# Gate and up products of a SwiGLU layer as seven block products instead of eight

## The chip, the cores and the metric

The kernel runs on one core of a Trainium2 chip. A core has a matrix engine (TensorE, in the profile PE, its weight loads PEld), three engines for element-wise work (VectorE or DVE, ScalarE or ACT, GpSimd or POOL), and queues that issue transfers (SP, and queues of ACT and POOL). Data lies in HBM, in the on-chip memory SBUF, and in PSUM, eight banks of 128 x 512 floats into which TensorE writes. The metric is the time of one execution on the device in microseconds (us).

## The reference

One decoder layer over 512 tokens of width 2048 in float32, then a norm:

```
h = rmsnorm(x, ln_mix);  proj = h @ w_in
mixed = [rmsnorm(stick_breaking(q, k, v)), rmsnorm(sliding_window(q, k, v, sinks))]
x = x + mixed @ w_out
h = rmsnorm(x, ln_ffn)
gate, up = split(h @ w_gate_up, 2)          # 2048 x 5632 each
x = x + (silu(gate) * up) @ w_down          # 5632 x 2048
out = rmsnorm(x, ln_final)
```

The change concerns the gate and up products and what lies around them; the attention groups are as they were.

## The kernel before

Every large product runs in three matmuls: both factors are split into a rounded part (hi) and the rest (lo), and hi x hi, hi x lo and lo x hi are added in PSUM. ScalarE writes hi (a copy, line 172 for weights), VectorE writes lo (a subtraction of hi from the raw value, line 173).

Weights come in slabs of 128 x 1024 from a queue. `step()` runs one group of three matmuls of the slab at its head; in the course of a slab it also loads the next two and splits the next one, so that transfers and splits lie under matmuls. `drain()` runs the queue to a mark, and `pull()` lets other work be woven in. `defer(n, fn)` runs a piece of work after n further groups. Loads go out through SP, pinned to written order; the order of the other engines' instructions is set by a scheduler that takes what is ready, with written order as priority. Each engine then takes its own instructions in that fixed order.

The stages: attention with its projections; the output projection in two halves (`add_outA`, `add_outB`), which leaves x2, the residual, in four column quarters in SBUF; then the feed-forward part. `h2_split(c)` transposes a quarter of x2 and splits it into hi and lo of the transposed tokens (lines 226 and 227). `add_up(n)` queues the gate and the up product of a group of 512 features (`add_wide`, lines 364 to 366: weight slab stationary, 512 tokens moving, 16 steps of contraction), reads the banks, applies the norm's factor per token and Silu, and splits the result (lines 896 to 906). `add_down(n)` multiplies the group before it with its down weights, and adds to x2 (line 916). The eleven groups alternate: up of group n, down of group n - 1. The last group's down product goes token tile by token tile, with the final norm behind it.

Of the kernel before, what the change touches and what calls it, by code (L numbers as in the profile page):

```python
# [8 lines left out]
F32 = mybir.dt.float32  # L9
# [28 lines left out]
def tile_hymba(ctx: ExitStack, tc: tile.TileContext, x, ln_mix, w_in, sb_norm, swa_norm,  # L38
# [7 lines left out]
    act = ctx.enter_context(tc.tile_pool(name="act", bufs=32))  # L46
    o8 = ctx.enter_context(tc.tile_pool(name="o8", bufs=2))
    v8 = ctx.enter_context(tc.tile_pool(name="v8", bufs=4))
    wp = ctx.enter_context(tc.tile_pool(name="wp", bufs=2))
    sm = ctx.enter_context(tc.tile_pool(name="sm", bufs=4))  # L50
    ps = ctx.enter_context(tc.tile_pool(name="ps", bufs=2, space=bass.MemoryType.PSUM))

# [83 lines left out]
    # Products with weights run from one queue of slabs [128, a, b] of a weight  # L136
    # (a*b = 1024), each split exactly in hi + lo ahead of its matmuls.
# [4 lines left out]
    def load(i):  # L142
# [4 lines left out]
        if sl["big"] is not None:  # L147
            # two slabs of one load
            if not sl["big"]:
                sl["big"].append(phase[1].tile([P, 2 * a, b], F32, tag="raw8", name="raw8", bufs=2))  # L150
# [31 lines left out]
    def step():  # L182
        """One group of matmuls of the queue; returns its time on the tensor engine."""
# [33 lines left out]
    carry = [0.0]  # L217

    def drain(mark=None):
        """To the end of slab number mark, or of the queue."""  # L220
# [23 lines left out]
    def row_bc(col, name):  # L244
# [6 lines left out]
        res = const.tile([P, S], F32, tag="rbc", name=name)  # L251
# [3 lines left out]
    # h^T = (x * g)^T, split  # L255
    h_hi = [None] * KT
    h_lo = [None] * KT
    XC = [(0, 256), (256, 256), (512, 512), (1024, 512), (1536, 512)]
# [13 lines left out]
    def h_make(kt):  # L272
# [4 lines left out]
        h_hi[kt] = act.tile([P, 512], F32R, tag="a", name="hhi")  # L277
        h_lo[kt] = act.tile([P, 512], F32R, tag="a", name="hlo")
# [48 lines left out]
    # queued products with features on the output partitions, 256 at a time  # L327
# [26 lines left out]
    # the same, 512 features at a time, in pairs of slabs of one load  # L354
# [30 lines left out]
    # V of the first head group, per key block [128 keys, head, hi | lo]  # L385
# [53 lines left out]
    def stack_two(src, r0, hi, lo):  # L439
        """[hi;hi] and [lo;lo] of the 64 rows of src from r0."""  # L440
# [581 lines left out]
```

## Time and profile before

| | |
|---|---|
| time, median of 3 runs | 2176.59 us (2175.39 to 2176.8) |
| profiled execution, first to last instruction | 2174.1 us; the page gives no other time of it |
| PE busy | 2156.3 us, 99% |
| DVE busy | 1040.6 us, 48% |
| ACT busy | 772.3 us, 36% |
| POOL busy | 131.1 us, 6% |
| moved by DMA | 208.18 MB, mean 96 GB/s |
| attention with its projections | about 0 to 590 us |
| end of output projection | about 725 us |
| gate, up and down products | about 725 to 2165 us |

Busy time is the union of an engine's instructions; matmuls overlap, so the pace of TensorE is read from the distance of their starts. A row of a group gives line, engine, operation, the output and inputs by the program's names, shapes and count, then the busy time in us with the mean of one in ns, and the time that the engine stood idle before them with what ended it. A row of a timeline gives start and duration in us.

### The profile page before, as it was taken

To read this page: it belongs to the slowest core of one execution; us is meant where nothing else is said; L and a number is where in the kernel's file an instruction comes from. 1 tells how busy PE (TensorE), PEld (TensorE's weight loads), DVE (VectorE), ACT (ScalarE), POOL (GpSimd) and SP (SyncE) were. 2 spreads that over 40 slices of the span, in tenths; PEclk is the share of its full clock that TensorE was granted. 3 is DMA by queue.
4 is the path that set the end of the run, shared out by engine and by line. 5 is a ranking of instruction groups with operands and counts; after the bars stand their busy time and mean duration, and the time that the engine had idled before them with its cause. 6 is when DMAs were issued, how large, how long until landed. Compare 5 with 4: busy or idle time off the path is not lost.

```text
span 2174.1 us, 24468 instructions
## 1 busy us (share of the span) xinstructions
PE 2156.3 (99%) x9930; PEld 1790.5 (82%) x9930; DVE 1040.6 (48%) x1521; ACT 772.3 (36%) x1277; POOL 131.1 (6%) x193
## 2 busy tenths in 40 slices
PE   8999999999999999999999999999999999999998
PEld 7888888988888888888888888888888888888886
DVE  4368888679834333433424334252333424334265
ACT  5347777468624322212222221222212222221232
POOL 0024444100100000000000000000000000000000
PEclk9999999999999999999999999999999999999999
DMA  5232221222333222222222222222222222222332
GB/s 182 90 88 59 68 68 59 78 77 79 136 116 115 69 97 97 97 97 97 97 97 97 97 97 97 97 97 97 97 97 97 97 97 97 97 97 97 107 126 78
DMA packets 136960, 208.18 MB, mean 96 GB/s; under 512 B 5072, under 2 KB 51216, under 8 KB 136720
## 3 DMA queue, kind: packets, MB, share of 16 engines
q1 hardware_dynamic: 136576, 205.54, 28.1%
q8 instruction: 78, 1.28, 0.2%
q0 software_dynamic: 176, 1.06, 0.1%
q14 instruction: 34, 0.28, 0.0%
q10 hardware_dynamic: 96, 0.02, 0.0%
HBM read 202.41 MB, written 4.19 MB: 95 GB/s over the span
## 4 chain that ended last, share of the span: by engine, by line
PE 98%; DVE 1%; ACT 0%; DMA 0%; issue 0%; SPq 0%; DVEq 0%
PE z L366 7%; PE z L364 7%; PE z L365 7%; PE m L337 4%; PE m L339 4%; PE m L338 4%; PE z L306 4%; PE z L305 4%; PE z L307 4%; PE m L305 4%; PE m L307 4%; PE o L366 4%; PE m L365 4%; PE m L366 4%; PE o L365 4%; PE o L364 4%
## 5 line engine op out<-in xcount | busy, mean ns | idle before, releaser
L173 DVE TENSOR_TENSOR wlo<-raw,whi 128x1024 fp32r<-128x1024 f32 x360 | 441.6, 1227 | 962.0 <-ACT whi L172 959.6
L172 ACT ACTIVATE whi<-raw 128x1024 fp32r<-128x1024 f32 x360 | 381.2, 1059 | 1152.6 <-PE o L365 325.9
L364 PE MATMUL z<-h2hi,whi 128*128 128x512 f32 x704 | 273.9, 389 | 0.0
L365 PE MATMUL z<-h2lo,whi 128*128 128x512 f32 x704 | 273.9, 389 | 0.0
L366 PE MATMUL z<-h2hi,wlo 128*128 128x512 f32 x704 | 273.9, 389 | 0.0
L337 PE MATMUL m<-hhi,whi 128*128 128x512 f32 x416 | 169.5, 407 | 0.9 <-DVE swv L227 0.9
L339 PE MATMUL m<-hhi,wlo 128*128 128x512 f32 x416 | 163.2, 392 | 0.0
L338 PE MATMUL m<-hlo,whi 128*128 128x512 f32 x416 | 163.2, 392 | 0.0
L365 PEld LDWEIGHTS z<-h2lo,whi 128*128 128x128 f32 x704 | 132.2, 188 | 27.5
L366 PEld LDWEIGHTS z<-h2hi,wlo 128*128 128x128 f32 x704 | 132.2, 188 | 27.4
L364 PEld LDWEIGHTS z<-h2hi,whi 128*128 128x128 f32 x704 | 132.2, 188 | 27.3
L364 PE MATMUL o<-h2hi,whi 128*128 128x512 f32 x352 | 137.1, 390 | 0.0
L364 PE MATMUL m<-h2hi,whi 128*128 128x512 f32 x352 | 137.1, 390 | 0.0
L366 PE MATMUL o<-h2hi,wlo 128*128 128x512 f32 x352 | 137.0, 389 | 0.0
L366 PE MATMUL m<-h2hi,wlo 128*128 128x512 f32 x352 | 136.9, 389 | 0.0
L365 PE MATMUL m<-h2lo,whi 128*128 128x512 f32 x352 | 136.9, 389 | 0.0
L365 PE MATMUL o<-h2lo,whi 128*128 128x512 f32 x352 | 136.9, 389 | 0.0
L305 PE MATMUL z<-whi,ah 128*128 128x512 f32 x320 | 124.5, 389 | 0.0
L306 PE MATMUL z<-wlo,ah 128*128 128x512 f32 x320 | 124.5, 389 | 0.0
L307 PE MATMUL z<-whi,al 128*128 128x512 f32 x320 | 124.5, 389 | 0.0
L339 PEld LDWEIGHTS m<-hhi,wlo 128*128 128x128 f32 x416 | 78.1, 188 | 17.7
L337 PEld LDWEIGHTS m<-hhi,whi 128*128 128x128 f32 x416 | 78.9, 190 | 11.0 <-PE z L745 1.1
(261 smaller groups left out, 3721.9 us busy)
## 6 DMA issues: line engine op xcount, KB each, us to landing
raw<-in_w_gate_up_dram SPq DMA_DIRECT2D x88, 1024.0 KB, 4.9
raw<-in_w_down_dram SPq DMA_DIRECT2D x40, 1024.0 KB, 5.1
raw<-in_w_in_dram SPq DMA_DIRECT2D x40, 512.0 KB, 3.5
raw<-in_w_in_dram SPq DMA_DIRECT2D x64, 256.0 KB, 3.2
raw<-in_w_out_dram SPq DMA_DIRECT2D x32, 512.0 KB, 3.6
x<-in_x_dram SPq DMA_DIRECT2D x4, 1024.0 KB, 6.8
raw<-in_w_down_dram SPq DMA_DIRECT2D x8, 512.0 KB, 6.1
out_dram<-x SPq DMA_DIRECT2D x16, 256.0 KB, 2.6
```

The source lines that it names most:

```text
L172: ih = A.activation(out=hi, in_=raw, func=AF.Copy)
L173: il = V.tensor_tensor(out=lo, in0=raw, in1=f(hi), op=ALU.subtract)
L305: mm(o, lhsT=lh[:, sl], rhs=hi[:, j, :], start=first, stop=False, skip_group_check=halves)
L306: mm(o, lhsT=lh[:, sl], rhs=lo[:, j, :], start=False, stop=False, skip_group_check=halves)
L307: mm(o, lhsT=ll[:, sl], rhs=hi[:, j, :], start=False, stop=(k == nslab * a - 1), skip_group_check=halves)
L337: mm(o, lhsT=wh, rhs=xh, start=(k == 0), stop=False)
L338: mm(o, lhsT=wh, rhs=xl, start=False, stop=False)
L339: mm(o, lhsT=wl, rhs=xh, start=False, stop=(k == KT - 1))
L364: mm(o, lhsT=wh, rhs=xh, start=(k == 0), stop=False)
L365: mm(o, lhsT=wh, rhs=xl, start=False, stop=False)
L366: mm(o, lhsT=wl, rhs=xh, start=False, stop=(k == KT - 1))
```

## The change

The matrix of tokens (512 x 2048) is cut into token halves and feature halves, the pair gate and up (2048 x 2 x 128 per unit of 128 features) into row halves and into gate and up. The 2 x 2 block product is formed from seven products of sums of blocks (the form of Winograd), named "1" to "7" and run in the order 1, 2, 5, 6, 3, 7, 4.

- Token side: `h2_split` now writes the transposed, scaled quarter unsplit (`xh`). `h_slab` forms the seven sums of token blocks for each of two slabs of 1024 features, some on VectorE and two on GpSimd, and `halves_of` splits each: hi of 256 tokens in columns 0 to 255, lo in 256 to 511 (`hc`). Slab 0 is made during the output projection, slab 1 during the first products.
- Weight side: a `Part` loads four blocks per unit (128 columns, 512 rows for each of two slabs), forms four sums of them on GpSimd (`sum`, two products ahead), splits each of the seven on ScalarE and VectorE (`split`, one ahead) and multiplies (`product`: 8 matmuls of 512 columns with hi, 8 of 256 columns with lo, into one bank). Unit 0 comes in two parts, one for each slab.
- `take` combines the seven banks in SBUF as they come, one product late; `finish` adds the halves (hi and lo columns) on GpSimd, applies factor and Silu, and stores 128 x 512 activations to HBM (`aT`).
- x2 goes to HBM (`x2s`) at the end of each quarter of the output projection, and comes back ahead of the down products, which now all follow the last unit. Activations are loaded by group and split again (`load_act`, `split_act`). The factor of the second norm is now in the activations.
- Tiles of 128 x 512 that were single are now held by fours (`act8`); pools of SBUF are closed and opened at the two borders of the stage.

The diff, cut to its core:

```diff
-    o8 = ctx.enter_context(tc.tile_pool(name="o8", bufs=2))
...
+    def act8(name, dt=F32R):
+        return act.tile([P, 4, 512], dt, tag="a8", name=name, bufs=8)
...
+    x2s = [dram.tile([P, NT, 512], F32, name=f"x2s{c}") for c in range(4)]
+    aT = [dram.tile([P, 4, 512], F32, name=f"aT{n}") for n in range(NFF // 4)]
+    xh = [None] * 4
+    hc = {}
...
     def h2_split(c):
+        xh[c] = (o8.tile([P, 4, 512], F32, tag="o8", name="xh") if c < 2 else e8("xh"))
         for k4 in range(4):
             kt = c * 4 + k4
             pb = pz()
             for t in range(NT):
                 nc.tensor.transpose(out=pb[:, t * P:(t + 1) * P], in_=x2[c][:, t, k4 * P:(k4 + 1) * P], identity=ident)
-            h2_hi[kt] = act.tile([P, 512], F32R, tag="a", name="h2hi")
-            h2_lo[kt] = act.tile([P, 512], F32R, tag="a", name="h2lo")
-            split_scaled(pb, gcol[:, 16 + kt:17 + kt], h2_hi[kt], h2_lo[kt])
+            V.scalar_tensor_tensor(out=xh[c][:, k4, :], in0=pb, scalar=gcol[:, 16 + kt:17 + kt], in1=rs1["b"],
+                                   op0=ALU.mult, op1=ALU.mult)
+    def halves_of(src, hl):
+        A.activation(out=hl[:, :, 0:256], in_=src, func=AF.Copy)
+        V.tensor_tensor(out=hl[:, :, 256:512], in0=src, in1=f(hl)[:, :, 0:256], op=ALU.subtract)
+    def h_blocks(s, a11, a21, a12, a22, stmp, new):
+        s1, s2 = stmp[:, 0], stmp[:, 1]
+        s4, s3 = s1, s2
+        def put(p, src):
+            hc[p, s] = new(p)
+            halves_of(src, hc[p, s])
+        put("1", a11)
+        yield
+        put("2", a12)
+        yield
+        V.tensor_tensor(out=s1, in0=a21, in1=a22, op=ALU.add)
+        put("5", s1)
+        yield
+        V.tensor_tensor(out=s2, in0=s1, in1=a11, op=ALU.subtract)
+        put("6", s2)
+        yield
+        G.tensor_tensor(out=s4, in0=a12, in1=s2, op=ALU.subtract)
+        put("3", s4)
+        yield
+        G.tensor_tensor(out=s3, in0=a11, in1=a21, op=ALU.subtract)
+        put("7", s3)
+        yield
+        put("4", a22)
+    def h_slab(s):
+        xa, xb = xh[2 * s], xh[2 * s + 1]
+        return h_blocks(s, xa[:, :, 0:256], xa[:, :, 256:512], xb[:, :, 0:256], xb[:, :, 256:512],
+                        e8("ssum").rearrange("p (u a) (h b) -> p u (a h) b", u=2, h=2),
+                        lambda p: act8("hca") if p not in "125" else
+                        side.tile([P, 4, 512], F32R, tag="s8", name="hcs", bufs=3) if s == 0 else
+                        ft("hct", [P, 4, 512], F32R, 3))
     def add_outB(c):
         def done(t, pb):
             xc = x2[c][:, t, :]
             V.scalar_tensor_tensor(out=xc, in0=pb, scalar=rstdB[:, t:t + 1], in1=xc, op0=ALU.mult, op1=ALU.add)
-            A.activation(out=tmp(name="junk"), in_=xc, func=AF.Square, accum_out=ss2[:, t, c:c + 1])
+            A.activation(out=junk, in_=xc, func=AF.Square, accum_out=ss2[:, t, c:c + 1])
             if t == NT - 1:
-                defer([6, 6, 38, 8][c], lambda: h2_split(c))
-                if c == 3:
-                    defer(9, rstd2_make)
+                dma(out=x2s[c], in_=x2[c])
+                if c < 3:
+                    defer(6, lambda: h2_split(c))
+                if c == 1:
+                    defer(12, lambda: list(h_slab(0)))
...
+    drain(outB0)
+    phase[0].close()
+    right = ExitStack()
+    side = right.enter_context(tc.tile_pool(name="side", bufs=1, side="right", reuse_waits="tile"))
+    drain()
...
+    class Part:
+        def __init__(self, unit, s0, s1):
+            self.u, self.s0, self.s1 = unit, s0, s1
...
+        def load(self, q):
+            r, c = int(q[0]) - 1, int(q[1]) - 1
+            raw = (wp.tile([P, 8, P], F32, tag="raw", name="raw", bufs=RAWB) if c == 0 else
+                   ft("raw2", [P, 8, P], F32, 3))
+            c0 = c * DFF + self.u.j * P
+            for s in range(self.s0, self.s1):
+                r0, k = s * 1024 + r * 512, 4 * (s - self.s0)
+                dma(out=raw[:, k:k + 4, :], in_=wgu[r0:r0 + 512, c0:c0 + P].rearrange("(a p) c -> p a c", p=P))
+            self.raw[q] = raw[:, 0:self.n, :]
+        def sum(self, p):
+            if p not in "5674":
+                return
+            t = ft("t", [P, 8, P], F32, 3)[:, 0:self.n, :]
+            a, b = {"5": ("12", "11"), "6": ("22", "T5"), "7": ("22", "12"), "4": ("21", "T6")}[p]
+            G.tensor_tensor(out=t, in0=self.raw[a], in1=self.t[b[1]] if b[0] == "T" else self.raw[b],
+                            op=ALU.subtract)
+            self.t[p] = t
+        def split(self, p):
+            src = self.t[p] if p in self.t else self.raw[{"1": "11", "2": "21", "3": "22"}[p]]
+            hi = wp.tile([P, 8, P], F32R, tag="whi", name="whi", bufs=2)[:, 0:self.n, :]
+            lo = wp.tile([P, 8, P], F32R, tag="wlo", name="wlo", bufs=2)[:, 0:self.n, :]
+            A.activation(out=hi, in_=src, func=AF.Copy)
+            V.tensor_tensor(out=lo, in0=src, in1=f(hi), op=ALU.subtract)
+            self.w[p] = hi, lo
+        def product(self, p):
+            if self.s0 == 0:
+                self.u.bank[p] = bank8()
+            b = self.u.bank[p]
+            hi, lo = self.w.pop(p)
+            for i in range(self.n):
+                x = hc[p, self.s0 + i // 4][:, i % 4, :]
+                mm(b, lhsT=hi[:, i, :], rhs=x, start=(self.s0 == 0 and i == 0), stop=False, skip_group_check=True)
+            for i in range(self.n):
+                x = hc[p, self.s0 + i // 4][:, i % 4, 0:256]
+                mm(b[:, 0:256], lhsT=lo[:, i, :], rhs=x, start=False,
+                   stop=(self.s1 == 2 and i == self.n - 1), skip_group_check=True)
+    class Unit:
+        def __init__(self, j):
...
+        def take(self, p):
+            b = self.bank
+            def plus(tile, bank, other):
+                V.tensor_tensor(out=tile, in0=bank, in1=other, op=ALU.add)
+                return tile
+            if p == "1":
+                self.w4 = e8("w4")
+                self.s1 = self.w4[:, 0, :]
+                A.activation(out=self.s1, in_=b["1"], func=AF.Copy)
+                self.c = e8("c4")
+            elif p == "2":
+                plus(self.c[:, 0, :], b["2"], self.s1)
+            elif p == "6":
+                self.u2 = plus(self.w4[:, 1, :], b["6"], self.s1)
+                self.u4 = plus(self.w4[:, 2, :], b["5"], self.u2)
+            elif p == "3":
+                plus(self.c[:, 2, :], b["3"], self.u4)
+            elif p == "7":
+                self.u3 = plus(self.w4[:, 3, :], b["7"], self.u2)
+                plus(self.c[:, 3, :], b["5"], self.u3)
+            elif p == "4":
+                plus(self.c[:, 1, :], b["4"], self.u3)
+                self.finish()
+        def finish(self):
+            g4 = e8("g4")
+            g, u, a = g4[:, 0, :], g4[:, 1, :], g4[:, 2, :]
+            G.tensor_tensor(out=g4[:, 0:2, :].rearrange("p a (h b) -> p (a h) b", h=2), in0=self.c[:, :, 0:256], in1=self.c[:, :, 256:512], op=ALU.add)
+            V.tensor_tensor(out=g, in0=g, in1=r2["b"], op=ALU.mult)
+            A.activation(out=g, in_=g, func=AF.Silu)
+            V.tensor_tensor(out=u, in0=u, in1=r2["b"], op=ALU.mult)
+            V.tensor_tensor(out=a, in0=g, in1=u, op=ALU.mult)
+            dma(out=aT[self.j // 4][:, self.j % 4, :], in_=a)
+    h2_split(3)
+    upper.close()
+    upper = ExitStack()
+    ff = upper.enter_context(tc.tile_pool(name="ff", bufs=1, reuse_waits="tile"))
...
...
+    first = {"1": ("11",), "2": ("21",), "5": ("12",), "6": ("22",)}
...
...
+    LD, SU = 7, 2
+    for n in range(LD):
+        ahead(n, "load")
+    for n in range(SU):
+        ahead(n, "sum")
+    ahead(0, "split")
...
+    for n, (pt, p) in enumerate(steps):
+        ahead(n + LD, "load")
+        ahead(n + SU, "sum")
+        ahead(n + 1, "split")
+        pt.product(p)
+        if n == 1:
+            late = h_slab(1)
+        if 2 <= n < 7:
+            next(late, None)
+            next(late, None)
+        if n == 7:
+            rstd2_make()
+        if taken:
+            u, q = taken.pop()
+            u.take(q)
+        if pt.s1 == 2:
+            taken.append((pt.u, p))
+    u, q = taken.pop()
+    u.take(q)
+    tc.keep_in_program_order(A.preload_act_table_set("natural_log_exp_and_others"))
+    upper.close()
+    right.close()
+    upper = ExitStack()
+    xp = upper.enter_context(tc.tile_pool(name="xp", bufs=1, reuse_waits="tile"))
+    side = upper.enter_context(tc.tile_pool(name="side2", bufs=1, side="right", reuse_waits="tile"))
...
+    def load_act(n):
+        raw = side.tile([P, GF, 512], F32, tag="ar", name="araw", bufs=2)
+        dma(out=raw, in_=aT[n])
+        acts[n] = raw
+    def split_act(n):
+        raw = acts[n]
+        ah = side.tile([P, GF, 512], F32R, tag="ah", name="ah", bufs=2)
+        al = side.tile([P, GF, 512], F32R, tag="al", name="al", bufs=2)
+        for h in range(2):
...
+            A.activation(out=ah[:, sl, :], in_=raw[:, sl, :], func=AF.Copy)
+            V.tensor_tensor(out=al[:, sl, :], in0=raw[:, sl, :], in1=f(ah)[:, sl, :], op=ALU.subtract)
+        acts[n] = ah, al
...
+    load_act(0)
+    split_act(0)
+    load_act(1)
+    for c in range(4):
+        x2[c] = xp.tile([P, NT, 512], F32, tag="x2", name="x2r", bufs=4)
+        nc.scalar.dma_start(out=x2[c], in_=x2s[c])
...
...
-    def add_up(n):
-        sg = [None] * GF
-        c0 = n * GF * P
-        def g_done(c, pb):
-            g = sg[c] = tmp(name="g")
-            V.tensor_tensor(out=g, in0=pb, in1=r2["b"], op=ALU.mult)
-            A.activation(out=g, in_=g, func=AF.Silu)
-        def u_done(c, pb):
-            if c == 0:
-                acts[n] = (o8.tile([P, GF, 512], F32R, tag="o8", name="ah"),
-                           phase[1].tile([P, GF, 512], F32R, tag="al", name="al", bufs=2))
-            ah, al = acts[n]
-            V.tensor_tensor(out=sg[c], in0=pb, in1=sg[c], op=ALU.mult)
-            A.activation(out=ah[:, c, :], in_=sg[c], func=AF.Copy)
-            V.tensor_tensor(out=al[:, c, :], in0=sg[c], in1=f(ah)[:, c, :], op=ALU.subtract)
-        add_wide(wgu, c0, next_four, g_done, h2T)
-        add_wide(wgu, DFF + c0, next_four, u_done, h2T)
     def add_down(n):
         for c in range(4):
             r0 = n * GF * P
             def done(t, pb, c=c):
                 xc = x2[c][:, t, :]
-                V.scalar_tensor_tensor(out=xc, in0=pb, scalar=r2["c"][:, t:t + 1], in1=xc,
-                                       op0=ALU.mult, op1=ALU.add)
+                V.tensor_tensor(out=xc, in0=pb, in1=xc, op=ALU.add)
             add_tok(lambda s, c=c: wdn[r0:r0 + GF * P, c * 512:(c + 1) * 512], GF // 2, 2, 512,
...
     def last_w(k2, c):
         raw = wp.tile([P, 2, 512], F32, tag="raw", name="raw", bufs=RAWB)
...
-        for e in range(2):
-            hi = act.tile([P, 512], F32R, tag="a", name="lhi")
-            lo = act.tile([P, 512], F32R, tag="a", name="llo")
-            A.activation(out=hi, in_=raw[:, e, :], func=AF.Copy)
-            V.tensor_tensor(out=lo, in0=raw[:, e, :], in1=f(hi), op=ALU.subtract)
-            lastw[2 * k2 + e, c] = (hi, lo)
-    # last norm: out = (x * g) * rstd
+        if k2 == 0:
+            lastw[c] = act8("lhi"), act8("llo")
+        hi, lo = (x[:, 2 * k2:2 * k2 + 2, :] for x in lastw[c])
+        A.activation(out=hi, in_=raw, func=AF.Copy)
```

More of the change, by code (lines that the diff above doesn't have):

```diff
@@ L250, in row_bc @@
                skip_group_check=True)
[L251 removed]
+        res = const.tile([P, S], F32, name=name)
         A.activation(out=res, in_=pb, func=AF.Copy)
@@ L965, in last_col @@
                 dma(out=o2d[t * P:(t + 1) * P, k * 512:(k + 1) * 512], in_=xc)
-    for n in range(1, NG):
-        add_up(n)
-        if n == NG - 1:
-            queue[-1]["post"] = last_up
+    for n in range(NG - 1):
+        if n == NG - 2:
             last_from = len(queue)
-        add_down(n - 1)
+        add_down(n)
     drain(last_from)
```

99 lines of the change are left out of this document (69 added, 30 removed).

## The prediction

> **What bounds the kernel now.** I read the page first, then the windows, the timelines of single engines, and the groups.
>
> ```profile
> span 2174.1 us, 24468 instructions
> PE 2156.3 (99%) x9930; PEld 1790.5 (82%) x9930; DVE 1040.6 (48%) x1521; ACT 772.3 (36%) x1277; POOL 131.1 (6%) x193
> PE 98%; DVE 1%; ACT 0%; DMA 0%; issue 0%; SPq 0%; DVEq 0%
> L173 DVE TENSOR_TENSOR wlo<-raw,whi 128x1024 fp32r<-128x1024 f32 x360 | 441.6, 1227 | 962.0 <-ACT whi L172 959.6
> L172 ACT ACTIVATE whi<-raw 128x1024 fp32r<-128x1024 f32 x360 | 381.2, 1059 | 1152.6 <-PE o L365 325.9
> L364 PE MATMUL z<-h2hi,whi 128*128 128x512 f32 x704 | 273.9, 389 | 0.0
> L364 PE MATMUL o<-h2hi,whi 128*128 128x512 f32 x352 | 137.1, 390 | 0.0
> L364 PE MATMUL m<-h2hi,whi 128*128 128x512 f32 x352 | 137.1, 390 | 0.0
> ```
>
> TensorE is the bound: 98% of the chain that ended last is its own. Lines 364 to 366 are the gate and up products, three matmuls of each kind, 3 x (704 + 352 + 352) = 4224. Their 389 ns overlap, so the pace must come from a stretch in which nothing else runs. The windows give it (columns: stretch, length, then busy time and count of PE, PEld, DVE, ACT, POOL, clock, DMA share, GB/s).
>
> ```profile
> 217.00:271.00 54.00, 54.00 (x272) 44.76 (x271) 47.42 (x83) 41.42 (x86) 22.31 (x33) 1.00 0.23 69
> 1000.00:1200.00 200.00, 200.00 (x884) 165.66 (x883) 77.89 (x85) 46.18 (x49) 0.00 (x0) 1.00 0.28 95
> 2170.00:2174.00 4.00, 0.00 (x0) 0.00 (x0) 0.00 (x0) 0.00 (x0) 0.00 (x0) 0.50 0.57 207
> ```
>
> 884 matmuls in 200 us are 226.2 ns each, at full clock. Gate and up therefore hold TensorE for 4224 x 0.2262 = 955.6 us. VectorE (DVE) is busy for 39% of that stretch and GpSimd (POOL) not at all.
>
> **TensorE's part of the change.** For each of the 44 units (128 gate and 128 up features) there are now seven products with 1024 of contraction. Each product is 8 matmuls of 512 columns (weight hi by token hi and lo) and 8 of 256 columns (weight lo by token hi). The narrow ones run in the shared projection of the sliding window's values.
>
> ```profile
> 411.00 0.28 PE L305 MATMUL m<-whi,hhi 128*128 128x256 f32 x1
> 411.12 0.28 PE L306 MATMUL m<-wlo,hhi 128*128 128x256 f32 x1
> ...
> 420.00 0.28 PE L305 MATMUL m<-whi,hhi 128*128 128x256 f32 x1
> 437.09 0.40 PE L338 MATMUL m<-hlo,whi 128*128 128x512 f32 x1
> 437.32 0.39 PE L339 MATMUL m<-hhi,wlo 128*128 128x512 f32 x1
> 437.55 0.28 PE L305 MATMUL m<-whi,hhi 128*128 128x256 f32 x1
> 437.67 0.28 PE L306 MATMUL m<-wlo,hhi 128*128 128x256 f32 x1
> ```
>
> From 411.00 to 420.00 lie 75 steps, 120 ns each, every one with its own weight load, and a change of width in between costs nothing. A product is 8 x 0.2262 + 8 x 0.120 = 2.77 us, a unit 19.39 us, all units 853.1 us. TensorE's term is 853.1 - 955.6 = -102.5 us. The down products (2112 matmuls) keep their number and shape.
>
> The Trainium skill, "TensorE: Matmul & The Clock Gate", section "Back-to-back issue gap", has N/2.4 + 2.5 ns for one matmul; that estimate is 215.8 and 109.2 ns here and would make this term -110.8 us. The rows are 10 ns slower each, and they decide.
>
> **What VectorE and GpSimd get.** Per unit VectorE subtracts seven weight slabs (L173's shape, 1.227 us), reads PSUM seven times (one bank, one tile of SBUF) and multiplies three times in SBUF. GpSimd forms four weight sums of 1024 elements and one add of halves of 1024. No row has 1024 elements on GpSimd; the minimum, median and maximum of its smaller ones, and VectorE's kinds, are:
>
> ```profile
> L595 POOL TENSOR_TENSOR af<-af,e x16: 738/839/1039, 139.5 to 389.8; 128x256 f32<-128x256 f32 x16
> L467 POOL TENSOR_TENSOR sqA<-sqA,oc x7: 1278/1299/1299, 212.9 to 403.4; 128x512 f32<-128x512 f32 x7
> L904 DVE TENSOR_TENSOR g<-z,g 128x512 f32<-128x512 f32 x44 | 30.2, 689 | 1.0
> L906 DVE TENSOR_TENSOR al<-g,ah 128x512 fp32r<-128x512 f32 x44 | 30.1, 686 | 0.0
> L897 ACT ACTIVATE g<-g 128x512 f32<-128x512 f32 x44 | 27.6, 628 | 28.5 <-DVE g L896 27.5
> ```
>
> 256 more elements cost 540 ns, so 1024 cost 1278 + 2 x 540 = 2.36 us. Alone, neither engine is a bound in 19.39 us: VectorE has 7 x 1.227 + 10 x 0.69 = 15.5 us, GpSimd 5 x 2.36 = 11.8 us, ScalarE 7 x 1.059 + 2 x 0.63 = 8.7 us. But the two first ones get in each other's way, as the timelines of the attention stage show (start, duration):
>
> ```profile
> 206.68 1.23 DVE L173 TENSOR_TENSOR wlo<-raw,whi 128x1024 fp32r<-128x1024 f32 x1 [0.42 <-ACT whi L172]
> 207.31 0.93 POOL L587 TENSOR_TENSOR ah<-e,e 128x128 fp32r<-128x128 f32 x1 [2.64 <-ACT e L615]
> 208.19 0.46 POOL L591 TENSOR_TENSOR af<-e,e 128x128 f32<-128x128 f32 x1
> 212.23 0.68 DVE L569 SCALAR_TENSOR_TENSOR e<-z,e 128x512 f32<-128x512 f32 x1
> 212.86 1.30 POOL L467 TENSOR_TENSOR sqA<-sqA,oc 128x512 f32<-128x512 f32 x1
> 213.60 1.10 DVE L575 TENSOR_TENSOR l<-e,h 128x512 fp32r<-128x512 f32 x1 [0.70 <-ACT h L570]
> 220.91 0.69 DVE L621 TENSOR_TENSOR l<-e,h 128x512 fp32r<-128x512 f32 x1
> 221.52 0.42 DVE L575 TENSOR_TENSOR l<-e,h 128x256 fp32r<-128x256 f32 x1
> ```
>
> At 213.60 a VectorE subtraction with both inputs in SBUF meets an add on GpSimd that ends at 214.16, and ends at 214.70: its own 0.69 us began at 214.01, 0.15 before the add's end. At 207.31 a GpSimd add meets line 173's subtraction (end 207.91); its own 0.46 us began at 207.78, 0.13 before. So such instructions run one after the other, whichever came first. The read of PSUM at 212.23 (z is a bank) ran 0.68 us under GpSimd adds, undisturbed. Of the new work per unit, the seven subtractions and three multiplies (7 x 1.227 + 3 x 0.69 = 10.66 us) and GpSimd's 11.8 us exclude each other: 22.45 us together, against TensorE's 19.39. Hand-overs give back 5 x 0.15 + 5 x 0.13, and VectorE behind itself 5 x 0.08 (0.69 long, next start after 0.61): 1.8 us. The floor is 20.65 us a unit, reached if every PSUM read lies under a GpSimd add. If none does, 7 x 0.61 = 4.27 comes on top: 24.9. These are the ends. VectorE takes its queue in order, so a PSUM read behind a waiting subtraction waits too; spread evenly, reads fall under GpSimd for half of the time (11.8 of about 23), which leaves 2.1 us, and 0.5 us goes where VectorE waits for the add of halves and then for Silu (0.63) with little else ready. I take 23.2 us, 44 x 23.2 = 1020.8 us: instead of -102.5 the stage becomes 1020.8 - 955.6 = +65.2 us. TensorE then waits some 3.8 us in each unit, for weights' lo or for sums.
>
> By the Trainium skill, "SBUF — State Buffer", section "Who interferes with whom", the loser "fully blocks" until the other has finished, with no hand-over gained: 22.05 us a unit and a floor of 970 us instead of 909. The rows show 0.13 to 0.15 us of overlap, so I keep 20.65.
>
> **The ends of the stage.** Today gate and up follow the output projection, and down products lie between them, without a gap. Now there are two joints.
>
> ```profile
> raw<-in_w_gate_up_dram SPq DMA_DIRECT2D x88, 1024.0 KB, 4.9
> raw<-in_w_in_dram SPq DMA_DIRECT2D x64, 256.0 KB, 3.2
> 14.00:20.00 6.00, 6.00 (x32) 5.05 (x31) 2.85 (x4) 4.25 (x13) 0.00 (x0) 1.00 1.05 387
> L227 DVE SCALAR_TENSOR_TENSOR h2lo<-z,gcol,h2hi 128x512 fp32r<-128x512 f32 x16 | 11.0, 744 | 4.9 <-ACT h2hi L226 4.8
> ```
>
> At the first, the SP queue is in written order: the store of the last quarter of x2 waits for the last PSUM read (0.75), and the first weights are behind it (256 KB, 3.2 us), then a hi copy (half of 1.059): 5 us, with the last transposes inside.
>
> In unit 0 the second slab's token blocks are made while TensorE works on the first slab. Exclusive are nine VectorE operations of 1.227, seven subtractions of 0.69 and four adds of 1.28 and two of 2.36 on GpSimd, 25.7 us together; TensorE needs the last block after 13 half products, 18 us: 7 us late, the PSUM work of 4 x 0.744 under it.
>
> At the second joint the last unit ends with a PSUM read 0.69, add 2.36, multiply 0.69, Silu 0.63, multiply 0.69: 5.1 us. Its store stands ahead of the loads of the first two activation groups and of the first down weights on SP: 4.9 us for the first MB and 2.7 for each further one at 387 GB/s, 10.3 us. A split (1.059 + 1.227) follows: 17.7 us, say 18. Bounds are 12 (weights beside the activations) and 28 (the 4 MB of x2 on ScalarE's queue come first, 10.6 us). The idle engine's clock fell to 0.50 in the last window above; on restart that may cost a few us, in the upper bound. Joints: 5 + 7 + 18 = 30 us, from 18 to 45.
>
> The rest is hidden. Weights and stores are 2.25 MB per unit in 256 KB pieces, 116 GB/s in 19.4 us; with the short rows of the 217 to 271 window (69 GB/s at 0.23) that is a share of 0.39. SP waits for the store of a unit early in the next, but loads lead by seven products. If that cover went, one 3.2 us landing per unit would show. Splitting activations (2.5 us of VectorE per 43 us group), the write and re-read of x2, and the down stage's DVE work lie under TensorE as now.
>
> **Sum.** The execution's span is 2174.1 us, 2.5 below the median 2176.6; I add the 2.5: 2176.6 + 65.2 + 30 = 2272 us.
>
> **Rivals.** (a) Faster, TensorE stays the bound: the two engines' collisions find room, because sums run ahead by three buffers and weights' lo is wanted only in a product's second half. Then -102.5, and joints of 5 + 2 + 18 = 25: 2099 us. For it: in the attention stage VectorE was 88% busy with GpSimd at 41% and TensorE had no gap (window 217 to 271). Against: it decides only while a unit's exclusive work stays under 19.39 us, and 20.65 is above that; GpSimd would have to need under 2.1 us for 1024 elements.
> (b) Perfect packing, 20.65 us: 909 - 955.6 = -47, plus 30: 2160 us. It needs every PSUM read under a GpSimd add, which an in-order queue rarely gives.
> (c) No packing and long joints: 24.9 x 44 = 1096, +140, plus 45: 2362 us.
> (d) The change doesn't do what it says, if the DMA can't feed it: at a share of 0.39 I give this nothing.
>
> **Chances.** Forecast 0.67, (a) 0.18, (b) 0.10, (c) 0.05. The forecast's own range, units of 21.7 to 24.5 us and joints of 20 to 40, is 2196 to 2339. To leave out no more than 2 in 10 the range must reach into (a): 2100 to 2340. A measurement of this kernel can tell about 0.2% (4.4 us) from nothing. Faster: (a) and 0.07 of (b), 0.25; same: 0.03 of (b) and 0.01 of the forecast's edge, 0.04; slower 0.71.
>
> **What would show it.** In the changed profile: matmuls at 226 and 120 ns within a product (right TensorE term); GpSimd adds of 1024 at about 2.36 us at best, subtractions of the weights well above 1.227 on the mean (right exclusion); TensorE's share falling to some 85% in the gate and up stage, with releasers on VectorE and ScalarE; units 22 to 24.5 us apart; a gap near 18 us ahead of the first down product, with DMA as releaser. The prediction is wrong if L173's successor keeps 1.23 us, or if units are 19.4 us apart.

## The result, and the profile after

The changed kernel takes 2293.24 us (median of 4 runs, 2290.52 to 2294.12) against 2176.53 (2175.39 to 2176.8) for the kernel before: a ratio of 1.0536, 95% interval 1.0521 to 1.0551. It is slower by 117 us. Forecast was 2272, with 2100 to 2340 as the range.

From the profile of the changed kernel come the span, the busy times and the costliest element-wise groups. L990 is the weights' lo in the new stage, L981 the weight sums, L1042 the add of halves, L1043 the multiply behind it; L178 is the old weights' lo outside the stage.

```profile
span 2291.3 us, 28101 instructions
PE 2112.4 (92%) x10634; PEld 1759.2 (77%) x10634; DVE 1648.0 (72%) x2002; ACT 926.1 (40%) x1428; POOL 798.6 (35%) x421
L178 DVE TENSOR_TENSOR wlo<-raw,whi 128x1024 fp32r<-128x1024 f32 x184 | 225.6, 1226 | 299.4 <-ACT whi L177 296.8
...
L990 DVE TENSOR_TENSOR wlo<-t,whi 128x1024 fp32r<-128x1024 f32 (+1 forms) x180 | 340.2, 1891 | 1.2 <-PE z L1003 1.1
...
L990 DVE TENSOR_TENSOR wlo<-raw,whi 128x1024 fp32r<-128x1024 f32 (+1 forms) x135 | 266.9, 1978 | 0.2 <-ACT whi L989 0.2
...
L1042 POOL TENSOR_TENSOR g<-c 128x1024 f32<-128x1024 f32 x44 | 138.5, 3148 | 15.1 <-DVE c L1018 15.1
...
L1043 DVE TENSOR_TENSOR g<-g,rbc 128x512 f32<-128x512 f32 x44 | 32.7, 742 | 124.2 <-POOL g L1042 124.2
```

TensorE fell from 99% to 92% of the span. The same subtraction takes 1226 ns outside the stage and, on the mean, 1891 to 1978 inside. Below are the instruction view of line 1042 (least, median and greatest duration in ns, first and last start), a stretch of the stage (columns as in the prediction), and what TensorE waited for (total, times, longest, in us):

```profile
L1042 POOL TENSOR_TENSOR g<-c x44: 2331/3371/3393, 782.9 to 1777.7; 128x1024 f32<-128x1024 f32 x44
```

```profile
1000.00:1200.00 200.00, 178.07 (x978) 149.06 (x977) 173.06 (x148) 71.61 (x78) 129.01 (x44) 0.99 0.41 107
```

```profile
PE z L1003 <- DVE wlo L990: 70.7, 48, 5.5
PE o L1003 <- DVE wlo L990: 28.4, 23, 2.7
PE m L1003 <- DVE wlo L990: 26.1, 23, 2.7
PE m L313 <- ACT whi L177: 23.3, 2, 21.4
```

Line 1042 runs once per unit. Its 44 starts lie between 782.9 and 1777.7 us, so a unit comes every 23.13 us. TensorE is busy for 89% of the stretch, and 125 us of its waits are for the weights' lo. The timeline (start, duration) shows how they come about:

```profile
1400.14 2.40 POOL L981 TENSOR_TENSOR t<-raw,raw 128x1024 f32<-128x1024 f32 x1 [5.23 <-DMA raw<-in_w_gate_up_dram]
1400.69 2.93 DVE L990 TENSOR_TENSOR wlo<-t,whi 128x1024 fp32r<-128x1024 f32 x1
1402.62 3.27 POOL L981 TENSOR_TENSOR t<-raw,t 128x1024 f32<-128x1024 f32 x1
1403.54 0.68 DVE L1018 TENSOR_TENSOR w<-z,w 128x512 f32<-128x512 f32 x1
...
1409.19 3.37 POOL L1042 TENSOR_TENSOR g<-c 128x1024 f32<-128x1024 f32 x1
...
1412.60 0.69 DVE L1043 TENSOR_TENSOR g<-g,rbc 128x512 f32<-128x512 f32 x1 [2.28 <-POOL g L1042]
...
1413.81 1.22 DVE L990 TENSOR_TENSOR wlo<-t,whi 128x1024 fp32r<-128x1024 f32 x1
...
1415.08 0.74 PE L1003 MATMUL o<-hcs,wlo 128*128 128x256 f32 x4 [1.65 <-DVE wlo L990]
```

The subtraction of 1400.69 meets the sum that ends at 1402.54, and itself ends only at 1403.62. The sum of 1402.62 meets that subtraction and takes 3.27 us in its turn. The read of PSUM at 1403.54 runs under that sum undisturbed (0.68). At 1412.60 VectorE had stood for 2.28 us behind the add of halves; the subtraction behind it came late, and TensorE waited 1.65 us for it.

The span is 117.2 us longer than before. By TensorE's rows, unit 0 takes 36.65 us (740.86 to 777.51) and the 43 other units 23.24 each (to 1776.7). Together that is 1036 us where gate and up took 955.6: +80. The wait ahead of the stage is 7.2 us, the one behind it 21.4 and 2.6 more at a slow clock. The remaining 5.7 us lie elsewhere, and where is not known.

### The profile page after: what moved, and what is told of

Same layout as the page of the kernel before. It is cut to its first block, busy times and chain, and to the rows that moved or that the text cites. A ratio compares the mean times of both kernels' runs of the same rounds, so it can differ in the third digit from the quotient of the medians.

```text
span 2291.3 us, 28101 instructions
## 1 busy us (share of the span) xinstructions
PE 2112.4 (92%) x10634; PEld 1759.2 (77%) x10634; DVE 1648.0 (72%) x2002; ACT 926.1 (40%) x1428; POOL 798.6 (35%) x421
## 5 line engine op out<-in xcount | busy, mean ns | idle before, releaser
L178 DVE TENSOR_TENSOR wlo<-raw,whi 128x1024 fp32r<-128x1024 f32 x184 | 225.6, 1226 | 299.4 <-ACT whi L177 296.8
L177 ACT ACTIVATE whi<-raw 128x1024 fp32r<-128x1024 f32 x184 | 194.4, 1057 | 443.6 <-PE o L315 233.6
L981 POOL TENSOR_TENSOR t<-raw,raw 128x1024 f32<-128x1024 f32 (+1 forms) x90 | 261.3, 2904 | 278.4 <-DMA raw<-in_w_gate_up_dram 215.7
L990 DVE TENSOR_TENSOR wlo<-t,whi 128x1024 fp32r<-128x1024 f32 (+1 forms) x180 | 340.2, 1891 | 1.2 <-PE z L1003 1.1
L989 ACT ACTIVATE whi<-t 128x1024 fp32r<-128x1024 f32 (+1 forms) x180 | 187.0, 1039 | 292.3 <-DVE wlo L990 188.4
L981 POOL TENSOR_TENSOR t<-raw,t 128x1024 f32<-128x1024 f32 (+1 forms) x90 | 260.1, 2890 | 121.7 <-issue 114.1
L990 DVE TENSOR_TENSOR wlo<-raw,whi 128x1024 fp32r<-128x1024 f32 (+1 forms) x135 | 266.9, 1978 | 0.2 <-ACT whi L989 0.2
L989 ACT ACTIVATE whi<-raw 128x1024 fp32r<-128x1024 f32 (+1 forms) x135 | 140.1, 1038 | 149.8 <-PE z L1000 45.5
L1000 PE MATMUL z<-hca,whi 128*128 128x512 f32 x688 | 177.3, 401 | 0.0
L1000 PEld LDWEIGHTS z<-hca,whi 128*128 128x128 f32 x688 | 127.2, 194 | 23.2
L1042 POOL TENSOR_TENSOR g<-c 128x1024 f32<-128x1024 f32 x44 | 138.5, 3148 | 15.1 <-DVE c L1018 15.1
L1043 DVE TENSOR_TENSOR g<-g,rbc 128x512 f32<-128x512 f32 x44 | 32.7, 742 | 124.2 <-POOL g L1042 124.2
```

The lines of the kernel that those rows point to most:

```text
L177: ih = A.activation(out=hi, in_=raw, func=AF.Copy)
L178: il = V.tensor_tensor(out=lo, in0=raw, in1=f(hi), op=ALU.subtract)
L981: G.tensor_tensor(out=t, in0=self.raw[a], in1=self.t[b[1]] if b[0] == "T" else self.raw[b], op=ALU.subtract)
L989: A.activation(out=hi, in_=src, func=AF.Copy)
L990: V.tensor_tensor(out=lo, in0=src, in1=f(hi), op=ALU.subtract)
L1000: mm(b, lhsT=hi[:, i, :], rhs=x, start=(self.s0 == 0 and i == 0), stop=False, skip_group_check=True)
```

## The experiments

Line numbers in the rows are those of the kernel that ran. In the three runs on the joints the lines of the stage stand three lower in the file: there L1045 is the add of halves and L1006 the narrow matmul.

**Without GpSimd.** The four weight sums and the add of halves go to VectorE.

```diff
-            G.tensor_tensor(out=t, in0=self.raw[a], in1=..., op=ALU.subtract)
+            V.tensor_tensor(out=t, in0=self.raw[a], in1=..., op=ALU.subtract)
...
-            G.tensor_tensor(out=g4[:, 0:2, :]..., in0=self.c[:, :, 0:256], in1=self.c[:, :, 256:512], op=ALU.add)
+            V.tensor_tensor(out=g4[:, 0:2, :]..., in0=self.c[:, :, 0:256], in1=self.c[:, :, 256:512], op=ALU.add)
```

> The four weight sums and the add of halves of each unit run on VectorE; GpSimd has nothing in the gate and up stage. Theory (VectorE and GpSimd exclude each other at SBUF): no collision is left, VectorE needs 7 x 1.15 + 5 x 1.15 + 7 x 0.61 + 3 x 0.61 = 19.9 us per unit by its pace, the subtractions of weights fall back to 1.23 us, units come 20 to 21 us apart instead of 23.2, total 2160 to 2195 us. Rival (VectorE simply has too much to do in too fixed an order): its work grows by 5.8 us a unit, units of 25 us or more, total above 2370 us.

Measured 2126.47 us (2126.32 to 2130.91), ratio to the kernel before 0.9778 (0.9762 to 0.9794): faster than both kernels, and 34 us below the expected 2160 to 2195. The same stretch, and two operations of VectorE:

```profile
1000.00:1200.00 200.00, 200.00 (x1144) 174.65 (x1143) 200.00 (x226) 86.82 (x92) 0.00 (x0) 1.00 0.48 125
```

```profile
1400.32 1.23 DVE L981 TENSOR_TENSOR t<-raw,t 128x1024 f32<-128x1024 f32 x1
1401.46 1.23 DVE L1042 TENSOR_TENSOR g<-c 128x1024 f32<-128x1024 f32 x1
```

A unit has 112 matmuls, and 1144 of them in 200 us make 19.58 us a unit. TensorE has no gap, and VectorE is full as well. The busier engine got more work, and a unit is 3.6 us shorter: a sum takes VectorE 1.14 us from start to start, but on GpSimd it keeps VectorE's two-input work out for up to 2.34. By starts (1.14 us for 1024 elements, 0.60 for 512) VectorE's 22 operations of a unit are 12 x 1.14 + 10 x 0.60 = 19.7 us, which is just about the whole unit.

**Without the sums, and with fills in their place.** Each of these two kernels ran once, and each leaves part of the computation out. In the first the four weight sums are not formed, and a raw block is split in their place; the add of halves stays on GpSimd. In the second GpSimd fills the tile of each sum three times with a constant instead of computing it.

```diff
-            if p not in "5674":
-                return
+            return
...
-            src = self.t[p] if p in self.t else self.raw[{"1": "11", "2": "21", "3": "22"}[p]]
+            src = self.t[p] if p in self.t else self.raw[{"1": "11", ..., "5": "12", "6": "22", "7": "12", "4": "21"}[p]]
...
-            G.tensor_tensor(out=t, in0=self.raw[a], in1=..., op=ALU.subtract)
+            for _ in range(3):
+                G.memset(t, 0.5)
```

> The four weight sums of each unit are left out (a raw block takes the place of each sum), so GpSimd only adds the halves. Theory (exclusion): 10.7 + 2.4 us of exclusive work per unit lie well under TensorE's 19.4, units 19.4 to 20 us apart, total 2125 to 2165 us. Rival 1 (VectorE's own work and the wait for the add of halves and Silu in its queue): that is all still there, units of 22 us or more, total above 2240 us. Rival 2 (GpSimd's sums come late for ScalarE's copies): as the theory, 2125 to 2165.

> Each weight sum is replaced by three fills of the same tile on GpSimd, so GpSimd stays busy about as long, and everything that waited for a sum waits for the fills, but nothing is read from SBUF; the sums' values are left out. Theory (exclusion, with a reading GpSimd): subtractions of weights at 1.23 us, units of 19.4 to 20.5 us, total 2125 to 2185 us. Rival 2 (the sums' lateness): as the changed kernel, 2270 us or more. If GpSimd excludes VectorE also when it only writes: 2250 us or more, with long subtractions.

Measured 2122.9 us without the sums, 2 under the expected range, and 2125.42 with the fills, inside its range. From the profile of the second:

```profile
PE 2070.2 (97%) x10634; PEld 1760.0 (83%) x10634; DVE 1419.0 (67%) x2002; ACT 931.1 (44%) x1428; POOL 787.0 (37%) x781
L982 POOL MEMSET t<- 128x1024 f32 (+1 forms) x540 | 500.2, 937 | 154.5 <-DVE wlo L990 134.4
L990 DVE TENSOR_TENSOR wlo<-t,whi 128x1024 fp32r<-128x1024 f32 (+1 forms) x180 | 216.9, 1206 | 2.9 <-ACT whi L989 1.8 <-PE z L1003 1.1
```

GpSimd is busy for 787 us, almost as long as in the changed kernel (798.6). Three fills of a tile take 2.8 us, about as long as a sum, and the subtractions are back at 1206 ns. So GpSimd's load is not the cause, but that GpSimd reads SBUF while VectorE reads two tiles of it. The Trainium skill, "SBUF — State Buffer", section "Who interferes with whom", says the same: a VectorE instruction with two SBUF inputs contends with a GpSimd instruction that reads SBUF, not with one that only writes it; this trace agrees.

Two other causes remain to be excluded. One is that the sums come late. The fills do not wait for the loaded blocks as the sums do, so this run alone does not settle it; but in the changed kernel ScalarE's copies wait for a sum only 8 times, 14.8 us in all. The other is VectorE's wait for the add of halves. It is 124.2 us in the changed kernel and still 101.3 us without the sums, where TensorE has no gap in the same stretch.

**Only the halves on VectorE.** The add of halves moves, the four sums stay on GpSimd (the second pair of lines of the first experiment). The run asks whether the two engines' operations simply add up.

> The changed kernel with the addition of the two feature halves moved from GpSimd to VectorE, and the four weight sums left on GpSimd. Theory of exclusion: in a unit the operations of GpSimd and those of VectorE with two inputs in SBUF add up. Changed kernel: 5 x 2.34 + 7 x 1.22 + 3 x 0.69 = 22.3 us, measured 23.14 to 23.24, so about 0.85 for the hand-overs. Here 4 x 2.34 + 8 x 1.22 + 3 x 0.69 = 21.2 and 0.85: 22.05 us a unit, 43 to 44 x 1.1 to 1.2 us less: 2240 to 2250 us. Rival, the late sum: VectorE waited 124 us in all for GpSimd's addition, and if this wait is the loss itself, most of it comes back: 2170 to 2200 us. Rival, VectorE's rate alone: it gets an operation more and the time does not fall, 2290 or above.

Measured 2331.99 us (2329.52 to 2337.72), ratio to the kernel before 1.0722 (1.0706 to 1.0738): 39 us more than the changed kernel, where 43 to 53 less were expected by addition. The theory that the operations simply add up fell, and so did the rival by which VectorE's wait for the add of halves is the loss. The time lies where the third reading, VectorE's rate alone, put it (2290 or above); but with all five operations on VectorE the kernel is faster, so its rate alone cannot be the reason. A stretch, the waits of TensorE from 1000 to 1400 us, a piece of the timeline, and line 1045, a multiply in SBUF:

```profile
1000.00:1200.00 200.00, 177.02 (x923) 149.78 (x921) 177.84 (x147) 69.54 (x75) 100.84 (x33) 0.93 0.36 95
```

```profile
PE z L1003 <- DVE wlo L990: 27.1, 14, 2.7
PE o L1003 <- DVE wlo L990: 10.8, 6, 2.7
PE m L1003 <- DVE wlo L990: 10.0, 5, 2.7
```

```profile
1218.20 3.42 DVE L1042 TENSOR_TENSOR g<-c 128x1024 f32<-128x1024 f32 x1
1220.50 3.37 POOL L981 TENSOR_TENSOR t<-raw,raw 128x1024 f32<-128x1024 f32 x1
1221.55 3.41 DVE L990 TENSOR_TENSOR wlo<-t,whi 128x1024 fp32r<-128x1024 f32 x1
...
1230.76 1.21 PE L1003 MATMUL z<-hca,wlo 128*128 128x256 f32 x8 [2.70 <-DVE wlo L990]
1231.81 3.37 PE L1000 MATMUL z<-hca,whi 128*128 128x512 f32 x8
```

```profile
L1045 DVE TENSOR_TENSOR g<-g,rbc x44: 678/2893/2900, 787.8 to 1826.2; 128x512 f32<-128x512 f32 x44
```

A unit takes 24.2 us here, though its exclusive work (the two-input operations of both engines, which cannot overlap) is 1.1 us less. While the sums run, the engines take turns, and in this piece of the timeline VectorE has an operation of its own to set against each sum. The moved add costs 3.42 us, and line 1045's multiply (684 ns in the changed kernel) 2893 ns at the median. In the changed kernel VectorE stands idle behind GpSimd's add for part of that time. TensorE's waits are 47.9 us in these 400 us, 45.2 in the changed kernel, but in 25 pieces instead of 35. Soon after the wait of 2.70 us eight wide matmuls take 3.37 us, where eight take 2.00 at full clock. That does not follow every such wait: one unit earlier, after 2.69 us, the next eight take 2.00. The clock is 0.93 in this stretch against 0.99. Per unit TensorE is busy for 177.02 / 200 x 24.2 = 21.4 us against 178.07 / 200 x 23.13 = 20.6, and idle for 2.8 against 2.5: most of the longer unit is TensorE's own time at the slower clock. That is read from these rows; no run separates clock from waits.

**Narrow products, sums on GpSimd or on VectorE.** Each product becomes 24 matmuls of 256 columns into half a bank, so that no add of halves is needed.

```diff
-                x = hc[p, self.s0 + i // 4][:, i % 4, :]
-                mm(b, lhsT=hi[:, i, :], rhs=x, ...)
+                for e in range(2):
+                    x = hc[p, self.s0 + i // 4][:, i % 4, e * 256:e * 256 + 256]
+                    mm(b[:, 0:256], lhsT=hi[:, i, :], rhs=x, ...)
...
-            G.tensor_tensor(out=g4[:, 0:2, :]..., op=ALU.add)
```

> Products as 24 matmuls of 256 columns, as in the run with narrow products and sums on VectorE, but the four weight sums stay on GpSimd; the add of halves is gone. TensorE 20.2 us per unit. Theory (exclusion): VectorE's 10.7 us of two-input work in SBUF and GpSimd's 9.4 us exclude each other, 20.1 less 1.6 of hand-overs, and half of 2.4 us of PSUM reads on top: 19.7 us, about TensorE's need, so units of 20.5 to 21.5 us and a total of 2165 to 2210 us, with subtractions of weights well above 1.23 us on the mean. Rival (only the add of halves and its chain held things up): 20.2 us, 2150 us, subtractions at 1.23 us.

> Sums on VectorE, and each product as 24 matmuls of 256 columns (hi x hi, hi x lo, lo x hi into the same 256 columns) instead of 8 of 512 and 8 of 256, so the add of halves is gone and every read of PSUM has half the size. TensorE then needs 7 x 24 x 0.120 = 20.2 us per unit, VectorE 7 x 1.15 + 4 x 1.15 + 7 x 0.34 + 3 x 0.61 = 16.9 us. Theory (exclusion): TensorE becomes the bound again, units of 20.2 to 20.6 us, total 2160 to 2185 us. Rival (VectorE's order): 22 us or more, above 2240 us.

Measured 2192.13 us in one run with the sums on GpSimd, and 2180.71 (2173.05 to 2184.46) with them on VectorE, ratio to the kernel before 1.0018 (1.0009 to 1.0027). Both times are as expected. The stretch of each, GpSimd first:

```profile
1000.00:1200.00 200.00, 194.75 (x1607) 192.92 (x1606) 184.80 (x162) 78.15 (x85) 112.03 (x39) 1.00 0.44 116
```

```profile
1000.00:1200.00 200.00, 196.46 (x1619) 194.90 (x1618) 161.67 (x202) 78.98 (x87) 0.00 (x0) 1.00 0.44 115
```

A unit of 168 matmuls takes 20.9 and 20.75 us, the second a little over the expected 20.6: 124 ns a matmul instead of 120, with the weight loads (PEld) at 96 and 97% of the stretch. By these two times GpSimd's sums cost some 11 us here, but the ten runs with the sums on VectorE spread over as much (2173 to 2184). With the sums on GpSimd the exclusive work, 4 x 2.34 and on VectorE 7 x 1.22 + 3 x 0.69, is 20.0 us and fits into TensorE's 20.8. In the changed kernel it is 22.3 against 19.5 and does not fit.

**The joints: which queue.** On top of the first experiment, the last store of x2 and the store of the last unit's activations go out by GpSimd's queue, so that SP's loads are no longer behind them. The second of the two edits:

```diff
...
-            dma(out=aT[self.j // 4][:, self.j % 4, :], in_=a)
+            if self.j < NFF - 1:
+                dma(out=aT[self.j // 4][:, self.j % 4, :], in_=a)
+            else:
+                nc.gpsimd.dma_start(out=aT[self.j // 4][:, self.j % 4, :], in_=a)
```

> Sums and halves on VectorE as in the first run (2126.5 us), and the two stores at the joints (last quarter of x2, activations of the last unit) issued by GpSimd's queue instead of SP's, so that the loads behind them on SP do not wait. Theory of the joints (SP's written order costs 3 to 5 us at the first, 5 us at the second): 2112 to 2121 us. Rival (the loads wait for memory or bandwidth, not for SP's order): 2124 to 2129 us.

Measured 2128.0 us (2126.63 to 2131.64), ratio 0.9782 (0.9766 to 0.9798), no change from 2126.47, as the rival had it: that the loads stand behind the stores on SP was not the cause. What SP waited for at the second joint (1605 to 1640 us), and SP's, GpSimd's and TensorE's own rows:

```profile
SPq L89 <- DVE g L1045: 11.4, 1, 11.4
SPq L89 <- DMA aT<-g: 9.5, 1, 9.5
```

```profile
1615.69 10.27 SPq L89 DMA_DIRECT2D araw<-aT  x2
...
1618.09 0.56 POOL L1053 DMA_DIRECT2D aT<-g  x1 [865.40 <-DVE g L1049]
...
1626.07 11.73 SPq L89 DMA_DIRECT2D raw<-in_w_down_dram  x3
...
1635.06 1.22 PE L313 MATMUL m<-whi,ah 128*128 128x512 f32 x2 [21.42 <-ACT whi L177]
```

The first activations' load went out at 1615.69, the second's 10 us later, when the last store had landed, and the first down weights only behind it. Group 1 had been stored long before, so the second load most likely waited for on-chip memory that the store still read; no run changed that memory alone.

The first joint stayed at 7.2 us too, although SP asked for the first gate and up weights at 712.94 us here and at 732.94 in the changed kernel. There it is ScalarE's order that shows, in the changed kernel's rows:

```profile
739.24 1.04 ACT L874 ACTIVATE hct<-ssum 128x1024 fp32r<-128x1024 f32 x1
740.19 1.13 ACT L989 ACTIVATE whi<-raw 128x512 fp32r<-128x512 f32 x2
```

The weights' hi copy starts as the third copy of token blocks ends, without a gap; no run moved it ahead of them.

**The joints: what is loaded first.** The first activation group is loaded and split before the last unit ends, into a tile of its own; the first down weights are the first load behind the stage; the second group and x2 come back in pieces between the first down products.

```diff
+        if n == NSTEP - 3:
+            ar0 = act8("ar0", F32)
+            dma(out=ar0, in_=aT[0])
...
+    load(down0)
+    load_x2(0)
+    defer(6, lambda: load_x2(1))
+    defer(8, lambda: load_act(1))
...
```

> As the run before, and the first activation group is loaded and split before the last unit ends, the first down weights go ahead of everything else on SP, and x2 and the second activation group come back in pieces as they are needed. The wait at the second joint (20.5 us) is then the last unit's PSUM read no longer, only one load of weights that starts under the last products: 0 to 8 us, and the clock does not fall. Total 2095 to 2108 us. Rival (memory: the weights' tile lies where the last unit's tiles lie, so the load can't start before the end): the wait stays above 10 us, total above 2112 us.

Measured 2114.27 us (2113.02 to 2115.68), ratio 0.9715 (0.9701 to 0.973): 13.7 us less than the run before, but 6 above the expected range. The first joint did not move (7.2 us). The second fell from 21.4 to 7.5, which is within the expected 0 to 8, but the clock fell behind it all the same. What was left there stood on ScalarE:

```profile
1618.97 0.63 ACT L1047 ACTIVATE g<-g 128x512 f32<-128x512 f32 x1 [4.85 <-issue]
1619.62 1.28 ACT L1112 ACT_TABLE_LOAD   x1
1620.91 2.00 ACT L177 ACTIVATE whi<-raw 128x1024 fp32r<-128x1024 f32 x2
```

The hi copy of weights (L177), which had been loaded by then, stood behind the last unit's Silu and a load of the activation table.

**The joints: what is split first.** Two slabs of down weights are loaded and split by instructions written ahead of the last unit's `take`, and the first activation group is loaded six products earlier.

```diff
+        if n == NSTEP - 1:
+            ah0, al0 = act8("ah0"), act8("al0")
...
+            s0 = [split_w(w0[0])]
...
+    s0.append(split_w(w0[1]))
     u, q = taken.pop()
     u.take(q)
```

> The run before this one on the joints (store of the last activation on GpSimd's queue, first activation group and first down weights loaded early) still had 7.5 us between the last product and the first down matmul: the split of the first down weights stood on ScalarE behind the last unit's Silu and behind a load of the activation table. Here the first two slabs of down weights are loaded and split by instructions that stand ahead of the last unit's sums, and the first activation group ahead of the last but one product's sums. If that order is all that is left, the gap falls to under 1.5 us and the half clock behind it (about 2.5 us) goes as well: 8 to 10 us less, 2104 to 2107 us. If the gap is held by a landing or by memory that is not yet free, the time stays at 2112 to 2116. If VectorE, full in the last unit, merely hands the delay on to the last products: 2108 to 2111.

Measured 2105.96 us (2104.78 to 2109.57), ratio to the kernel before 0.9685 (0.9669 to 0.9701), as expected. TensorE's rows at the joint:

```profile
1611.52 1.11 PE L1006 MATMUL m<-hca,wlo 128*128 128x256 f32 x8
...
1612.89 0.63 PE L313 MATMUL o<-whi,ah 128*128 128x512 f32 x2
1614.38 0.50 PE L314 MATMUL m<-wlo,ah 128*128 128x512 f32 x1 [0.87 <-DVE wlo L1081]
1614.72 0.39 PE L315 MATMUL m<-whi,al 128*128 128x512 f32 x1
1614.95 0.39 PE L313 MATMUL m<-whi,ah 128*128 128x512 f32 x1
```

0.87 us are left of 21.4, and the matmuls behind it soon run 0.23 us apart, at full clock. This is the fastest version found: 3.2% below the kernel before.

## Why the prediction was right, and where it was not

- **The forecast** named the right case: TensorE stops being the bound, because two-input operations of VectorE and GpSimd exclude each other. The signs it named are there: subtractions far above 1.227 us, TensorE at 89% in the stage (some 85 predicted), a GpSimd add of 2.331 us at best (2.36), units 23.13 us apart (23.2). One sign differs: the gap ahead of the down products is 21.4 us and ends with a copy on ScalarE, which itself had waited for a load. The fills show the mechanism, and the first experiment its price. Of the 21 us by which the forecast was short, the joints are 15 and the unexplained rest 6.
- **The way to 23.2** is less sound than its hit. It added exclusive work, hand-overs and half of the PSUM reads between a floor and a ceiling. It has TensorE wait 3.8 us in each unit; 2.5 were measured, and a granted clock of 0.97 to 0.99 in the stage, which the sum leaves out, makes up part of the difference. That the unit came within 0.1 us is therefore in part luck. The hand-overs are there: the subtraction that starts at 1400.69 and ends at 1403.62 has 1.22 us of its own, which began 0.14 before the sum ended. The words "fully blocks", which the prediction quotes from the Trainium skill, "SBUF — State Buffer", section "Who interferes with whom", stand there on VectorE's 2-port modes; of two SBUF inputs the section says "contends". The move of the halves alone shows that such a sum does not forecast a step of 1 us: it made the sum smaller and the unit longer. What the runs support is the floor: where exclusive work fits into TensorE's unit (no sums, 13.0 against 19.5 us; narrow, 20.0 against 20.8) the stage goes at or near TensorE's pace. Where it does not, the order of VectorE's instructions probably decides what stands behind a sum; no run changed that order alone.
- **TensorE's term**, -102.5 us, was a little too large. In the runs without a gap a unit takes 19.50 (fills) to 19.58 us, not 19.39: -94 to -98 us. The step that failed is that a change of width in between costs nothing: in the changed kernel's timeline it is 1.85 us from the first of eight wide matmuls to the first narrow one, not 1.81.

```profile
1402.67 2.00 PE L1000 MATMUL m<-hca,whi 128*128 128x512 f32 x8
1404.52 1.11 PE L1003 MATMUL m<-hca,wlo 128*128 128x256 f32 x8
1405.47 1.09 PE L1000 MATMUL m<-hcs,whi 128*128 128x512 f32 x4
```

- **The joints** were the mis-sized term: 30 us predicted, 44.6 measured, which is at the very end of the stated 18 to 45. The parts, with the prediction in brackets, are 7.2 us (5), unit 0 with 13.4 us over a steady one (7), and 24.0 (18). Unit 0 is only 27.0 us with the sums on VectorE, 7.4 over a steady one: the other 6 us went with GpSimd's sums. At both joints the step that failed is that the store stands ahead of the loads on SP: moving the stores to another queue gained nothing. At the first joint the rows show ScalarE's copies of token blocks ahead of the weights' copy. At the second joint the runs show in its place a load that waits for the last store to land, with the weights behind it, and then ScalarE's order. The slow clock behind the gap was left to the upper bound and is real: 13 matmuls in 6 us, at a granted clock of 0.50.

```profile
1798.00:1804.00 6.00, 5.67 (x13) 3.98 (x14) 2.36 (x2) 1.19 (x2) 0.00 (x0) 0.50 0.57 176
```

- **The rivals.** That TensorE stays the bound (2099) was wrong for this kernel. Its mechanism holds for the one without GpSimd's sums, though not its time (2126); 2105.96 comes near it once the second joint is gone. Its condition, "under 2.1 us for 1024 elements" on GpSimd, was never met: the work had to leave GpSimd. Perfect packing (2160) did not occur. Of the last rival (2362), the long joints of 45 us came and the unpacked units of 24.9 us did not. DMA fed the stage, as said: a share of 0.41, 0.48 at full pace.

## What to carry to other kernels

An idle engine is free only if its work does not keep another engine waiting. Here GpSimd's reads of SBUF kept out VectorE's operations with two SBUF inputs, so such work on GpSimd should be priced as time on both engines; where VectorE does it in half the time, it may be cheaper there although VectorE looks full. At a border between stages, look for the load or split that stands behind the last result of the old stage, in its queue, its engine or its memory, and write it ahead. In these runs an add-up of exclusive work told whether the stage would be bound by it, and not by how much.

## What was not expected of the hardware

- The exclusion hangs on GpSimd's reads, which the prediction did not say: GpSimd fills of the same tiles, busy for nearly as long as the sums, left VectorE's subtractions at 1206 ns.
- A stream of 256-column matmuls with a weight load each ran at 124 ns a matmul with the loads busy for 96 to 97% of the time, where eight narrow ones between wide ones take 0.95 us, 119 ns each.
- The clock fell after waits of no more than 2.7 us each, though not after every one: in the kernel with only the halves moved it is 0.76 on the mean from 1229 to 1235 us. The Trainium skill, "TensorE: Matmul & The Clock Gate", section "Part 1: The HAM clock gate (the "warmup" mystery)", has the clock halved after at least one idle window of some 3.4 us; the longest wait of this kernel between 1000 and 1400 us is 2.7, so the trace does not agree with that sentence as far as idle means no matmul at all.

```profile
1229.00:1235.00 6.00, 4.24 (x17) 3.54 (x18) 5.26 (x6) 1.06 (x1) 0.00 (x0) 0.76 0.67 185
```
